# LN1's g and b behind the transpose, FFN2's sums made of turned tiles, the last rows by column halves, in an order written by hand

## The chip, the cores and the metric

The kernel runs on one core of a Trainium2 chip. A core has five engines with a queue of instructions each: TensorE (PE; its weight loads are shown apart as PEld), VectorE (DVE), ScalarE (ACT), GpSimd (POOL) and SyncE (SP), which issues the DMAs here. Engines run side by side and wait for each other through semaphores. The metric is the device time of one execution in microseconds (us).

## The reference

One layer of an encoder over x of 1024 tokens by 1024 columns, all float32: a half-step FFN, then attention and a two-directional state-space scan (SSD) side by side, then a second FFN, then a gated embedding. Each step ends in a layer norm.

```python
def _layer_norm(x, g, b):
    mu = jnp.mean(xf, axis=-1, keepdims=True)
    var = jnp.mean(jnp.square(xf - mu), axis=-1, keepdims=True)
    return (xf - mu) * lax.rsqrt(var + LN_EPS) * g + b
...
x = _layer_norm(ALPHA * x + 0.5 * _swiglu(x, ffn1_w_in[i], ffn1_w_out[i]), ln_g[i, 0], ln_b[i, 0])
...
y = y.reshape(B, S, SSD_WIDTH) * jax.nn.silu(z)
y = _rms(y.reshape(B, S, G, SSD_WIDTH // G), 1.0).reshape(B, S, SSD_WIDTH)
mix = jnp.concatenate([att_out, y * ssd_norm[i]], axis=-1) @ w_out[i]
x = _layer_norm(ALPHA * x + mix, ln_g[i, 1], ln_b[i, 1])
x = _layer_norm(ALPHA * x + 0.5 * _swiglu(x, ffn2_w_in[i], ffn2_w_out[i]), ln_g[i, 2], ln_b[i, 2])
e = p[i] @ ple_w[i]
gate = jax.nn.sigmoid(x @ ple_gate_w[i] + ple_gate_b[i])
return _layer_norm(ALPHA * x + gate * e, ln_g[i, 3], ln_b[i, 3])
```

`_swiglu(x, w_in, w_out)` is `(silu(x @ gate) * (x @ up)) @ w_out` with 2816 hidden columns.

## The kernel before

The tokens are eight row tiles of 128. A float32 matrix product is made of three products of halves: each operand is split into a high part (a cast on ACT) and a low part (the difference, on DVE: `lo`, line 87), and TensorE adds hi x hi, lo x hi and hi x lo in PSUM (`mm3`, line 116). So every operand of a product costs one ACT and one DVE operation, and one product of 128x512 over four blocks is 12 matmuls.

The stages, in order of time: FFN1 (its in-products and its out-product), the projections, attention, the right scan (`ssd_right`), the left scan (`ssd_left`, line 1342), then LN1 and FFN2's in-products, FFN2's out-product (`ffn_strassen`, line 414), and the gate with LN3.

The left scan runs over eight chunks. For each, `load` brings y (the right scan's half, from DRAM) and silu(z); the state adds its part; y is gated, normed and, a few steps later, transposed by `turn` (four 128x128 transposes, line 1363) and split, as the second half of the input of W_out. Between the chunks stand "fillers": `resident(t)`, the attention half of W_out for rows 3 to 7, and `mixed(t)`, the SSD half (`out_proj`, two products of 128x512, line 1402) with LN1 of that row tile. `mixed(0)` to `mixed(4)` lie in the scan or right behind it, `mixed(5)` to `mixed(7)` among the work for FFN2. LN1 of a row tile is: statistics (on DVE, or on ACT by `ln_stats_act`), a root (on POOL, `ln_root`, line 175), and `ln_apply` (line 183): two DVE passes over 128x1024, with g and with b, which are held as 128x1024 tiles, the same in each partition. The result is stored to DRAM as y2, which FFN2's residual reads back later, and stays in `acc[t]` for FFN2.

FFN2's in-product is made in Strassen's way (Winograd's form) on 2x2 blocks. Rows 0 to 3 of x and rows 4 to 7 are the block rows, columns 0 to 511 and 512 to 1023 the block columns. Beside the plain blocks B11, B21 and B22 it needs sums T1 to T4 of blocks, all transposed and split. Before the change, `turn_blocks` transposes (line 237, into PSUM) first the plain blocks of rows 0 to 3, later the sums, which `Sums` makes on DVE out of rows of `acc` (lines 1639 to 1647), each sum of 128x512 with four transposes of its own. Hidden columns come in 22 blocks f; each has seven products: two "first" ones (with B11 and B21, which need only rows 0 to 3: `ffn_first`), and five of the "rest" (with T2, T1, T3, T4, B22: `ffn_rest`). The first products of f = 0, 1, 2 run ahead, between the rows. The weight sums of a block (`mixed_sums`, four of 128x512) are on DVE for f = 0 and on POOL for the others, and in each rest two sums of results (u2 and p5) are on POOL.

TensorE runs in the order in which the program is written. The other engines' order is a scheduler's, by its own estimates, except inside `in_order(...)`, where it is the written one, and `behind(...)`, which puts work behind what is already there. Waits lie at the head of each engine's queue.

The out-product `ffn_strassen` runs seven products of 22 steps; each step multiplies one hidden tile, whose splits run some tiles ahead on ACT and DVE. Pieces of DVE work (`todo`) are handed out two a step from step 3 on.

Of the kernel before, what the change touches and what calls it, by code (L numbers as in the profile page):

```python
# [36 lines left out]
class Layer:  # L37
# [62 lines left out]

    def split_into(self, b, src, n=512, eng=None):
        self.nc.scalar.copy(out=b[:, 0, :n], in_=src)  # L102
# [59 lines left out]
    def ln_stats_act(self, a, junk):

        nc = self.nc
        st = self.small.tile([P, 4, 6], F32, name="ln_st")[:, 0, 0:4]
        k = self.small.tile([P, 8], F32, name="ln_k")
        nc.scalar.activation(out=a, in_=a, func=AF.Identity, accum_out=st[:, 0:1])
        nc.scalar.mul(st[:, 1:2], st[:, 0:1], -1.0 / D)
        for i in range(2):
            nc.scalar.activation(out=junk, in_=a[:, i * 512:(i + 1) * 512], func=AF.Square, bias=st[:, 1:2], accum_out=st[:, 2 + i:3 + i])  # L170
        nc.vector.tensor_scalar(out=k[:, 0:1], in0=st[:, 0:1], scalar1=1.0 / D, scalar2=None, op0=ALU.mult)
        nc.vector.tensor_tensor(out=k[:, 1:2], in0=st[:, 2:3], in1=st[:, 3:4], op=ALU.add)
        return self.ln_root(a, k, k[:, 1:2], 1.0 / D)
# [53 lines left out]
    def put(self, X, name, k, c, src):  # L227
        hi, lo = X[name]
        self.nc.scalar.copy(out=hi[:, k, c], in_=src)
        self.lo(lo[:, k, c], src, hi[:, k, c])  # L230

    def turn_blocks(self, X, *blocks):

        ps = self.psb().rearrange("p (u k t) -> p u k t", u=2, t=P)
        for u, (_, _, src) in enumerate(blocks):
            for k in range(4):
                self.nc.tensor.transpose(out=ps[:, u, k], in_=src[:, k * P:(k + 1) * P], identity=self.ident)
        for u, (name, t, _) in enumerate(blocks):
            self.put(X, name, slice(0, 4), slice((t % 4) * P, (t % 4 + 1) * P), ps[:, u])
# [7 lines left out]
    def mixed_sums(self, g, u, tmp, G):  # L247

        a11, a12, a21, a22 = g[:, :512], g[:, 512:], u[:, :512], u[:, 512:]
        s1, s2, s3, s4 = (tmp.tile([P, 512], F32, name=f"s{i + 1}") for i in range(4))  # L250
# [3 lines left out]
        G.tensor_tensor(out=s4, in0=a12, in1=s2, op=ALU.subtract)
# [5 lines left out]
    def ffn_first(self, X, tmp, sg, g, between=None, mid=None, end=None):  # L260

        p1 = tmp.tile([P, 512], F32, name="p1")
        w = g if isinstance(g, list) else self.gate_blocks(g)
# [3 lines left out]
        for i, b in enumerate(("B11", "B21")):  # L270
# [1535 lines left out]
```

## Time and profile before

| | us |
|---|---|
| median of 3 runs | 1994.98 (1994.54 to 1996.11) |
| profiled run | 1995.66 |
| span of the profiled run | 1993.9 |
| mean granted TensorE clock | 0.996 of full speed |
| left scan | about 1138 to 1202 of the span |
| rows 5 to 7, sums, first rests of FFN2 | about 1202 to 1309 |
| FFN2's out-product | about 1680 to 1894 |

In the rows of the profile a line number is that of the kernel before; `out<-in` gives the names of the tiles without their numbers; `[2.07 <-DVE y L1392]` behind a row says that the engine had been idle for 2.07 us and what ended the wait. TensorE is busy for 98% of the span, so only few stretches show it idle; the longest of them are in the two middle rows of the table.

### The profile page before, as it was taken

How to read it: one execution, taken by the hardware profiler on the slowest of the kernel's cores; microseconds unless marked ns; L12 is line 12 of the kernel's file. 1: busy time of each engine (PE TensorE's matmuls, PEld its weight loads, DVE VectorE, ACT ScalarE, POOL GpSimd, SP SyncE). 2: the span in 40 equal slices, each digit the busy share in tenths (PEclk: the TensorE clock that was granted, in tenths of full speed). 3: DMA queues.
4: the chain of work that ended last, by engine and by line, in shares of the span. 5: the costliest groups of instructions: out<-in, count | busy, mean ns of one | idle time of the engine just before them, and what ended most of it. 6: DMA issues, size and time to landing. Idle time of an engine off the chain costs nothing.

```text
span 1993.9 us, 25875 instructions
## 1 busy us (share of the span) xinstructions
PE 1954.4 (98%) x9244; PEld 1622.9 (81%) x9244; DVE 1536.6 (77%) x2306; ACT 863.7 (43%) x1499; POOL 467.6 (23%) x338
## 2 busy tenths in 40 slices
PE   8999999999999999999999998899999999999998
PEld 7788888888888889877888877778888888888886
DVE  7977777766668668759997789877778777567698
ACT  6433333334444235448887664433333333443311
POOL 0544445430001131000001011354445441001011
PEclk9999999999999999999999999999999999999999
DMA  7434544559864202230003471234454447976122
GB/s 286 143 122 153 189 176 147 186 190 358 296 232 148 85 21 95 78 132 7 1 1 123 164 259 64 85 122 166 157 185 164 170 164 257 381 254 226 43 74 95
DMA packets 146605, 308.90 MB, mean 155 GB/s; under 512 B 17345, under 2 KB 30017, under 8 KB 146476
## 3 DMA queue, kind: packets, MB, share of 16 engines
q1 hardware_dynamic: 146476, 307.25, 43.8%
q8 instruction: 72, 1.18, 0.2%
q14 instruction: 57, 0.47, 0.1%
HBM read 215.77 MB, written 91.42 MB: 154 GB/s over the span
## 4 chain that ended last, share of the span: by engine, by line
PE 83%; DVE 10%; DMA 3%; issue 2%; ACT 2%; POOL 1%; SPq 0%; DVEq 0%; POOLq 0%; ACTq 0%
PE sm L116 48%; PE big L490 12%; PE sm L490 9%; PE big L116 3%; PE big L1102 2%; PE sm L1124 2%; DVE blk L87 2%; PE sm L1139 1%; PE sm L1140 1%; DMA wr<-in_wo_dram 1%; DVE nm L1109 1%; PE sm L1317 1%; DVE xl L87 1%; DMA wT<-wr 1%; PE sm L1213 1%
## 5 line engine op out<-in xcount | busy, mean ns | idle before, releaser
L116 PE MATMUL sm<-xh,blk 128*128 128x512 f32 x1424 | 439.8, 389 | 0.0
L116 PEld LDWEIGHTS sm<-xh,blk 128*128 128x128 f32 x1424 | 267.5, 188 | 55.3
L116 PE MATMUL sm<-xl,blk 128*128 128x512 f32 x736 | 284.6, 390 | 0.0
L116 PE MATMUL sm<-blk,xl 128*128 128x512 f32 (+2 forms) x784 | 238.2, 371 | 0.2 <-ACT xn_t L955 0.2
L116 PE MATMUL sm<-blk,xh 128*128 128x512 f32 (+2 forms) x584 | 203.8, 380 | 0.1
L87 DVE TENSOR_TENSOR blk<-raw,blk 128x512 fp32r<-128x512 f32 (+1 forms) x174 | 175.0, 1015 | 36.0 <-ACT blk L102 35.4
L102 ACT CAST blk<-raw 128x512 fp32r<-128x512 f32 (+1 forms) x174 | 104.6, 611 | 216.7 <-PE sm L116 119.9
L179 POOL TENSOR_TENSOR ln_k<-ln_k,mhalf 128x1 f32<-128x1 f32 x32 | 39.8, 1248 | 591.2 <-DVE ln_k L178 590.3
L87 DVE TENSOR_TENSOR blk<-s,blk 128x512 fp32r<-128x512 f32 x176 | 152.5, 872 | 28.6 <-ACT blk L102 28.1
L102 ACT CAST blk<-s 128x512 fp32r<-128x512 f32 x176 | 107.2, 622 | 137.4 <-PE sm L116 113.0
L116 PEld LDWEIGHTS sm<-blk,xl 128*128 128x128 f32 x784 | 142.8, 188 | 24.2 <-ACT xn_t L955 0.5
L116 PEld LDWEIGHTS sm<-xl,blk 128*128 128x128 f32 x736 | 138.3, 188 | 29.2 <-DVE u L370 0.4
L490 PE MATMUL big<-xh 128*128 128x512 f32 x576 | 138.8, 390 | 0.0
L251 POOL TENSOR_TENSOR s<-raw 128x512 f32<-128x512 f32 x41 | 62.0, 1512 | 323.7 <-DVE blk L87 272.0
L87 DVE TENSOR_TENSOR xh<-blk,xh 128x1024 fp32r<-128x1024 f32 x78 | 95.3, 1222 | 51.2 <-ACT xh L438 40.6
L87 DVE TENSOR_TENSOR xl<-blk,xl 128x1024 fp32r<-128x1024 f32 x76 | 92.8, 1221 | 47.2 <-ACT xl L438 39.6
L490 PEld LDWEIGHTS big<-xh 128*128 128x128 f32 x576 | 107.8, 188 | 22.2
L438 ACT CAST xh<-blk 128x1024 fp32r<-128x1024 f32 x78 | 82.2, 1054 | 100.8 <-PE big L490 37.6
L116 PEld LDWEIGHTS sm<-blk,xh 128*128 128x128 f32 x584 | 109.8, 188 | 19.7 <-DVE blk L87 0.5
L438 ACT CAST xl<-blk 128x1024 fp32r<-128x1024 f32 x76 | 80.1, 1054 | 104.4 <-PE big L490 38.5
L490 PE MATMUL big<-xl 128*128 128x512 f32 x480 | 115.7, 390 | 0.0
L116 PE MATMUL sm<-xET2h,blk 128*128 128x512 f32 x352 | 109.8, 394 | 1.8 <-DVE blk L87 1.8
(330 smaller groups left out, 4066.0 us busy)
## 6 DMA issues: line engine op xcount, KB each, us to landing
raw<-in_wi_dram SPq DMA_DIRECT2D x84, 512.0 KB
blk<-hS SPq DMA_DIRECT2D x154, 256.0 KB
hS<-h SPq DMA_DIRECT2D x88, 256.0 KB
wr<-in_wo_dram SPq DMA_DIRECT2D x44, 512.0 KB
blk<-wT SPq DMA_DIRECT2D x88, 256.0 KB
hS<-sg SPq DMA_DIRECT2D x66, 256.0 KB
wT<-wr SPq DMA_DIRECT2D x66, 256.0 KB
blk<-in_wo_dram SPq DMA_DIRECT2D x66, 256.0 KB
```

Source lines behind the costliest of these rows:

```text
L87: (eng or self.nc.vector).tensor_tensor(out=out, in0=full, in1=hi.bitcast(F32), op=ALU.subtract)
L102: self.nc.scalar.copy(out=b[:, 0, :n], in_=src)
L116: self.nc.tensor.matmul(ps, lhsT=a, rhs=b, start=(i == 0), stop=(i == n - 1))
L179: nc.gpsimd.tensor_tensor(out=r, in0=v, in1=self.mhalf[:, :1], op=ALU.pow)
L251: G.tensor_tensor(out=s1, in0=a21, in1=a22, op=ALU.add)
L438: A.copy(out=b[:, :, 0], in_=r)
L490: nc.tensor.matmul(ps[q], lhsT=b[:, 0, x, cut], rhs=b[:, 1, y], start=j == i == 0, stop=j == NP - 1 and i == 2)
L1102: nc.tensor.matmul(ps[:, n * 512:(n + 1) * 512], lhsT=Q[:, h, q0:q0 + P], rhs=K[:, h // 4, j, n * 512:(n + 1) * 512], start=j == 0, stop=j ...
L1109: nc.vector.tensor_reduce(out=nm, in_=ps, axis=AX.X, op=ALU.max, negate=True)
L1124: nc.tensor.transpose(out=pt[:, k], in_=pr[:, kk * P:(kk + 1) * P], identity=self.ident)
L1139: nc.tensor.matmul(po, lhsT=vw, rhs=pth[k // 4][:, k % 4], start=k == 0, stop=False)
L1140: nc.tensor.matmul(po, lhsT=vw, rhs=ptl[k // 4][:, k % 4], start=False, stop=k == KD - 1)
```

## The change

1. LN1 no longer multiplies by g and adds b on rows. `Row.shift` is one ACT pass (scale and shift by the row's own factors); the rows go to DRAM so.
2. `flip(t)` transposes two raw rows at once (rows 6 and 7 alone), and ACT's eviction out of PSUM carries g and b, which are one number per partition there (`gT`, `bT`), eight pieces of 128x256 for a pair. The turned tiles overwrite `acc[t]` and `acc[t + 1]`.
3. All blocks and sums are then made of turned tiles in SBUF (`plain`, `Sums`), with no transpose of their own: 64 transposes of 128x128 in place of 112.
4. What was stored without g and b gets them in FFN2's out-product (`affine`: 32 operations of 128x512 on DVE, in the steps of products 1 to 3), out of 128x1024 tiles that are now loaded there.
5. Statistics are on DVE for all rows. Rows 5, 6 and 7 run by column halves: 5 left, 5 right, 6 left, 7 left, 6 right, 7 right.
6. ACT's and DVE's order from row 5 to the third first product is written by hand. The sums u2 and p5 of f = 0 and the weight sums of f = 1 move from POOL to DVE.
7. In the left scan, y of chunks 0 and 1 is loaded ahead, and a `turn` comes behind the next chunk's state steps.
8. The attention stage's reciprocal of 128x512 is cut in four.

```diff
@@ ln
+    def ln_shift(self, a, k):
+        self.nc.scalar.activation(out=a, in_=a, func=AF.Identity, scale=k[:, 6:7], bias=k[:, 7:8])
+
+    def ln_factors(self, k):
+        V = self.nc.vector
+        mv, r, h, t, s, m = k[:, 0:2], *(k[:, i:i + 1] for i in range(3, 8))
+        V.scalar_tensor_tensor(out=t, in0=r, scalar=h, in1=r, op0=ALU.mult, op1=ALU.mult)
+        V.scalar_tensor_tensor(out=s, in0=t, scalar=1.5, in1=r, op0=ALU.add, op1=ALU.mult)
+        V.scalar_tensor_tensor(out=m, in0=mv[:, 0:1], scalar=-1.0, in1=s, op0=ALU.mult, op1=ALU.mult)
@@ ffn_strassen
+        made_of = {1: ("11",), 2: ("12",), 3: ("21", "22")}
...
-            todo = [(t, i, q) for t, i in adds[p] for q in range(4)]
+            todo = [do for to in made_of.get(p, ()) for do in affine(*C[to])]
+            todo += [lambda a=(t, i, q): add(*a) for t, i in adds[p] for q in range(4)]
@@ ffn_y
+        def affine(t0, m):
...
+            for t in range(t0, t0 + 4):
+                for gb, op in zip(xgb, (ALU.mult, ALU.add)):
+                    yield lambda a=acc[t][:, m], gb=gb, op=op: V.tensor_tensor(out=a, in0=a, in1=gb[:, m], op=op)
@@ z_last
-            V.reciprocal(e, e)
+        def invert(m):
+            V.reciprocal(e[:, m], e[:, m])
@@ ssd_left
         load(0)
+        load(1)
         waiting = []
         for ch in range(NT):
-            if ch < NT - 1:
-                load(ch + 1)
...
                 st = self.next_state(two, st, 0, ch, xb)
+            if len(waiting) > 2:
+                turn(*waiting.pop(0))
+            if 0 < ch < NT - 1:
+                load(ch + 1)
...
-            if len(waiting) > 2:
-                turn(*waiting.pop(0))
@@ layer
-        lnp = self.load_ln(1, lp)
+        gT, bT = (self.const.tile([P, KD], F32, name=n) for n in ("gT", "bT"))
...
+        def flip(t, n=2, to=None):
...
+            for u in range(n):
+                for k in range(KD):
+                    nc.tensor.transpose(out=ps[k // 4][:, k % 4, u * P:(u + 1) * P], in_=acc[t + u][:, k * P:(k + 1) * P], identity=self.ident)
+            for k in range(KD):
+                nc.scalar.activation(out=to[k // 4][:, k % 4], in_=ps[k // 4][:, k % 4], func=AF.Identity, scale=gT[:, k:k + 1], bias=bT[:, k:k + 1])
...
-            self.ssd_left(c, loaded, late, mixT, fillers + [lambda: mixed(3), lambda: mixed(4)])
+            self.ssd_left(c, loaded, late, mixT, fillers + [lambda: mixed(3), lambda: (flip(0), mixed(4))])
...
-            plain(0)
-            plain(1)
-            mixed(5)
-            plain(2)
-            plain(3)
-            mixed(6)
-            sums(4)
-            apply7 = mixed(7)
-            sums(5)
+            flip(2)
...
+            with self.in_order(mybir.EngineType.Activation, mybir.EngineType.DVE):
+                plain(0)
+                plain(2)
...
+                r6.half(1)
+                r6.root()
+                flip(4)
+                later(*lo1)
+                r6.factors()
+                r6.shift()
+                r7.half(1)
+                r7.root()
...
+                t14 = s[4].one()
+                r7.factors()
+                r7.shift()
+                t24 = s[4].two()
+                t15 = s[5].one()
+                t25 = s[5].two()
+                p0 = first(w0, lambda: None)
+                later(*lo2, t24, t25, t14)
+                pre.append(self.first_kept(tmp, sgs[0], p0))
+                flip(6, 1, [acc[6][:, m] for m in (lo, hi)])
...
+                p1 = first(w1, lambda: flip(7, 1, [acc[7][:, m] for m in (lo, hi)]))
...
+                in_turn([s[t].three for t in range(4, NT)])
...
+                in_turn([s[t].four for t in range(4, NT)])
```

What this does to the order is best seen at three places. First, SP's queue ahead of the left scan, before (`acc1<-y1` brings back rows 0 to 2, `y2<-yd` the scan's y; ln_g and ln_b are LN1's two 128x1024 tiles):

```order
L1589 DMA acc1_10887<-y1_9639 128x1024
L1589 DMA acc1_10959<-y1_9639 128x1024
L148 DMA ln_g_10279<-in_ln_g_dram 128x1024
L149 DMA ln_b_10280<-in_ln_b_dram 128x1024
L1355 DMA y2_10288<-yd_9641 128x512
L1355 DMA y2_10292<-yd_9641 128x512
```

and with the change:

```order
L1622 DMA acc1_10887<-y1_9642 128x1024
L1622 DMA acc1_10959<-y1_9642 128x1024
L1385 DMA y2_10288<-yd_9644 128x512
L1385 DMA y2_10292<-yd_9644 128x512
L1385 DMA y2_10384<-yd_9644 128x512
L1385 DMA y2_10462<-yd_9644 128x512
L1220 DMA xb_10547<-xbn_6850 128x768
```

The two broadcast tiles are gone from here; they now stand in FFN2's out-product. Second, DVE around the statistics of row 7 (`acc1_10660`), before (xt2 is a sum of row 5, the `big` tiles are PSUM, `blk` the low parts of weights):

```order
L157 BN_STATS ln_st_11350<-acc1_10660 128x6
L178 TENSOR_SCALAR ln_k_11276<-ln_k_11276 128x1
L87 TENSOR_TENSOR xET3l_11127<-big_11376,xET3h_11126 128x4x128
L159 BN_AGGR ln_k_11353<-ln_st_11350 128x2
L180 TENSOR_SCALAR ln_k_11276<-ln_k_11276 128x1
L87 TENSOR_TENSOR xET2l_11125<-big_11362,xET2h_11124 128x4x128
L178 TENSOR_SCALAR ln_k_11353<-ln_k_11353 128x1
L193 SCALAR_TENSOR_TENSOR ln_k_11276<-ln_k_11276 128x1
L190 SCALAR_TENSOR_TENSOR acc1_10660<-acc1_10660,ln_k_11353,ln_g_10279 128x512 x2
L87 TENSOR_TENSOR xl10_11133<-big_11376,xh10_11132 128x4x128
```

and with the change:

```order
L1440 SCALAR_TENSOR_TENSOR acc1_10660<-sm_11350,acc1_10660 128x512
L167 BN_STATS ln_st_11208<-acc1_10660 128x6
L171 BN_AGGR ln_k_11365<-ln_st_11208 128x2
L177 TENSOR_SCALAR ln_k_11365<-ln_k_11365 128x1
L179 TENSOR_SCALAR ln_k_11365<-ln_k_11365 128x1
L1696 TENSOR_TENSOR acc1_10785<-acc1_10404,acc1_10785 128x4x128
L193 SCALAR_TENSOR_TENSOR ln_k_11365<-ln_k_11365 128x1
L194 SCALAR_TENSOR_TENSOR ln_k_11365<-ln_k_11365 128x1
L195 SCALAR_TENSOR_TENSOR ln_k_11365<-ln_k_11365 128x1
L1696 TENSOR_TENSOR u3_11376<-acc1_10482,acc1_10785 128x512
```

The wide passes with ln_g have gone, and the sums T1 and T2 of rows 4 and 5 (line 1696) now stand behind row 7's statistics. Third, DVE around the low parts of T4 (`xl11`), which the fourth product of the first rest reads, before (L1647 is the last of the sums T4; the two rows that follow the last one here repeat it for the right half):

```order
L276 TENSOR_TENSOR sg_11148<-p1_11517,sm_11550 128x512
L1647 TENSOR_TENSOR acc1_10296<-acc1_10296,xt2_11507 128x512
L87 TENSOR_TENSOR blk_11579<-s3_11511,blk_11579 128x512
L87 TENSOR_TENSOR blk_11582<-blk_11144,blk_11582 128x512
L363 TENSOR_TENSOR u2_11603<-p1_11391,sm_11606 128x512
L87 TENSOR_TENSOR blk_11585<-s4_11512,blk_11585 128x512
L87 TENSOR_TENSOR xl11_11390<-big_11620,xh11_11389 128x4x128
L87 TENSOR_TENSOR xl11_11390<-big_11633,xh11_11389 128x4x128
```

and with the change (L1696 are the sums T4):

```order
L87 TENSOR_TENSOR blk_11551<-s3_11246,blk_11551 128x512
L87 TENSOR_TENSOR blk_11554<-s4_11247,blk_11554 128x512
L1696 TENSOR_TENSOR acc1_10887<-acc1_10887,u3_11376 128x4x128
L1696 TENSOR_TENSOR acc1_10887<-acc1_10887,u2_11377 128x4x128
L372 TENSOR_TENSOR u2_11584<-p1_11422,sm_11587 128x512
L87 TENSOR_TENSOR xl11_11197<-acc1_10887,xh11_11196 128x4x128
L1696 TENSOR_TENSOR acc1_10296<-acc1_10296,h3_11487 128x4x128
L87 TENSOR_TENSOR xl11_11197<-acc1_10887,xh11_11196 128x4x128
L1696 TENSOR_TENSOR acc1_10296<-acc1_10296,p5_11488 128x4x128
L378 TENSOR_TENSOR u3_11585<-u2_11584,sm_11623 128x512
L87 TENSOR_TENSOR xl11_11197<-acc1_10296,xh11_11196 128x4x128 x2
L87 TENSOR_TENSOR xl10_11151<-acc1_10482,xh10_11150 128x4x128 x2
```

The low parts read SBUF (`acc1`) where they read PSUM (`big`) before; two of T4's four come behind `u3`, which needs the T3 product, and the low parts of B22 (`xl10`) follow.

More of the change, by code (lines that the diff above doesn't have):

```diff
@@ L157, in ln_stats, with ln_part, ln_rest @@
             nc.vector.bn_stats(st[:, i], a[:, i * size:(i + 1) * size])
+        return self.ln_rest(st, a)
+    def ln_part(self, st, a, i):
+        self.nc.vector.bn_stats(st[:, i], a[:, i * 512:(i + 1) * 512])
+    def ln_rest(self, st, a):
         k = self.small.tile([P, 8], F32, name="ln_k")
-        nc.vector.bn_aggr(k[:, 0:2], st)
+        self.nc.vector.bn_aggr(k[:, 0:2], st)
         return self.ln_root(a, k, k[:, 1:2], 1.0)
[L162 to L173, printed above, removed]
     def ln_root(self, a, k, var, scale):
@@ L227, in put, with put_later @@
     def put(self, X, name, k, c, src):
+        self.put_later(X, name, k, c, src)()
+    def put_later(self, X, name, k, c, src):
         hi, lo = X[name]
         self.nc.scalar.copy(out=hi[:, k, c], in_=src)
[L230 to L239, printed above, removed]
+        return lambda: self.lo(lo[:, k, c], src, hi[:, k, c])
     def product(self, w, x):
@@ L1400, in ssd_left, with out_proj @@
             turn(*w)
-    def out_proj(self, t, half, wm, mixT, a):
+    def out_proj(self, t, half, wm, mixT, a, ns=(0, 1)):
         nc = self.nc
-        for n in range(2):
+        for n in ns:
             m = slice(n * 512, (n + 1) * 512)
@@ L1700, in run, with __init__, one, two @@
-            lctx.close()
-            tmp.more()
+                def __init__(s, t, t2):
+                    s.t, (s.a12, s.a22), (s.a11, s.a21), s.t2 = t, F[t], F[t - 4], t2.rearrange("p (k t) -> p k t", t=P)
+                def one(s):
+                    sub(s.a11, s.a12, s.a11)
+                    return put("T1", s.t, s.a11)
+                def two(s):
+                    sub(s.t2, s.a22, s.a11)
+                    return put("T2", s.t, s.t2)
+                def three(s):
+                    sub(s.a12, s.a22, s.a12)
+                    return put("T3", s.t, s.a12)
@@ new lines, in four, with last, in_turn, gate @@
+                def four(s):
+                    sub(s.a21, s.a21, s.t2)
+                    return put("T4", s.t, s.a21)
+                def last(s):
+                    return put("B22", s.t, s.a22)
+            def in_turn(steps):
+                waiting = None
+                for step in steps:
+                    do = step()
+                    if waiting:
+                        waiting()
+                    waiting = do
+                waiting()
+            def gate(g):
+                return zip(*[self.split_later(g[:, m]) for m in (lo, hi)])
@@ L1702, in run, with rests @@
+            blocks0 = [blocks0[i] for i in range(5)]
+            g1, u1 = w(1, 0), w(1, 1)
+            mark = []
+            def rests():
+                with self.behind(mybir.EngineType.Activation), self.behind(mybir.EngineType.DVE):
+                    in_turn([s[t].last for t in range(4, NT)])
+                mark.append(self.last(mybir.EngineType.DVE))
             hS, store = self.left_factors(1, tmp)
-            self.ffn_rest(X, tmp, lambda h: store(0, h), blocks0, *pre[0], between=last_sums)
+            self.ffn_rest(X, tmp, lambda h: store(0, h), blocks0, *pre[0], between=(rests,), G=V)
@@ L1707, in run @@
             _, wT, steps = self.right_sums(xc, 1, I["wo2"])
-            self.ffn_h(X, I["wi2"], tmp, store, pre, 1, steps)
+            self.ffn_h(X, I["wi2"], tmp, store, pre, 1, steps, mark[0], (g1, u1))
         with ExitStack() as c:
             rctx.close()
-            acc, xT, wg, tp, turn = self.ffn_y(c, 2, lambda t: y2[t], hS, I["wo2"], wT, [I["wg"][0, k] for k in range(4)])
+            acc, xT, wg, tp, turn = self.ffn_y(c, 2, lambda t: y2[t], hS, I["wo2"], wT, [I["wg"][0, k] for k in range(4)], xln=1)
             self.gate(c, xT, turn, acc, wg, self.load_ln(3, tp, ("s1", "s2")))
```

210 lines of the change are left out of this document (123 added, 87 removed).

## The prediction, on record before the run

> **What bounds the kernel now.** I first read the page: engine totals and the shares of the chain that ended last.
>
> ```profile
> PE 1954.4 (98%) x9244; PEld 1622.9 (81%) x9244; DVE 1536.6 (77%) x2306; ACT 863.7 (43%) x1499; POOL 467.6 (23%) x338
> PE 83%; DVE 10%; DMA 3%; issue 2%; ACT 2%; POOL 1%; SPq 0%; DVEq 0%; POOLq 0%; ACTq 0%
> ```
>
> TensorE sets the time; what can be won is its waits, its slow clock and its own instructions. So I next read the busy times by window for the stretch that the change rewrites (columns: window, us, busy time and count of PE, PEld, DVE, ACT, POOL, then TensorE's granted clock, DMA share, GB/s), with one window of FFN2's out-product for comparison.
>
> ```profile
> 1155.00:1202.00 47.00, 44.82 (x203) 36.91 (x202) 42.06 (x106) 26.70 (x98) 6.39 (x8) 0.96 0.60 202
> 1202.00:1256.00 54.00, 48.15 (x244) 39.02 (x242) 53.47 (x117) 26.02 (x59) 7.51 (x8) 1.00 0.17 69
> 1256.00:1287.00 31.00, 26.77 (x131) 22.31 (x132) 21.52 (x34) 12.50 (x23) 6.04 (x5) 0.94 0.23 85
> 1287.00:1309.00 22.00, 19.45 (x84) 15.48 (x83) 20.67 (x22) 9.39 (x15) 17.68 (x12) 0.99 0.37 120
> 1309.00:1330.00 21.00, 21.00 (x87) 17.19 (x86) 18.05 (x23) 8.17 (x14) 10.93 (x8) 0.93 0.43 151
> 1700.00:1750.00 50.00, 50.00 (x222) 41.42 (x221) 31.64 (x35) 24.04 (x27) 0.00 (x0) 1.00 0.99 365
> ```
>
> Between 1155 and 1309 PE idles 47.00 - 44.82 + 54.00 - 48.15 + 31.00 - 26.77 + 22.00 - 19.45 = 14.8 us, and VectorE is full there (53.47 of 54, 20.67 of 22). Third, the waits of PE from 1205 to 1320, grouped (in total, times, longest), and one row of the chain of waits at the worst of them, the store that the sum waits for:
>
> ```profile
> PE big L237 <- DVE xt L1644: 7.1, 4, 2.5
> PE sm L116 <- DVE sg L371: 2.6, 2, 2.3
> PE big L237 <- DVE acc L1640: 1.3, 2, 0.7
> PE sm L1363 <- DVE y L1392: 1.2, 1, 1.2
> ...
> 1253.72 2.64 DMA y<-acc
> ```
>
> 8.4 of these 12.4 us are transposes that wait for the sums of LN1's rows (xt, acc): row, statistics, LN1, store, sum, transpose, in a chain that lies on DVE. Before them stands one wait in the left scan. These rows also mark the ends of my sum:
>
> ```profile
> 1161.98 1.08 PE L1363 MATMUL sm<-ident,y 128*128 128x128 f32 x4 [2.07 <-DVE y L1392]
> 1201.36 0.60 PE L1363 MATMUL sm<-ident,y 128*128 128x128 f32 x4
> 1270.65 0.47 PE L116 MATMUL sm<-xET2l,blk 128*128 128x512 f32 x1 [0.24 <-issue]
> 1308.57 0.68 PE L116 MATMUL sm<-xET2l,blk 128*128 128x512 f32 x1 [2.29 <-DVE sg L371]
> ```
>
> 1201.36 is the transpose of scan chunk 5; 1308.57 is the first product (T2) of the third FFN2 block's rest. **All sums below go against the profiled run, 1995.66 us (span 1993.9 and 1.8 around it); the median of the three runs, 1994.98, is 0.7 lower.** About 0.2% (4 us) is what a measurement of this kernel can tell from no change.
>
> **The change, part by part.** *Left scan.* The 1 MB of broadcast g and b leaves the queue ahead of the scan's y loads, and the first turn goes behind two more steps of the scan:
>
> ```profile
> 1145.16 0.33 SPq L148 DMA_DIRECT2D ln_g<-in_ln_g_dram  x1
> 1145.54 0.43 SPq L149 DMA_DIRECT2D ln_b<-in_ln_b_dram  x1
> 1146.01 3.22 SPq L1355 DMA_DIRECT2D y<-yd  x4
> ```
>
> That is worth what the window 1155 to 1202 loses: 2.18 us idle and 0.04 x 47 = 1.9 us of clock (0.96). Taken: 4.1; bounds 0 (the wait only moves) and 4.1.
>
> *PE's work from chunk 5's transpose to the third rest.* I price it by pitch, from start to start:
>
> ```profile
> 1215.75 1.91 PE L237 MATMUL big<-ident,acc 128*128 128x128 f32 x16
> 1217.41 0.48 PE L116 MATMUL sm<-blk,xh 128*128 128x512 f32 x1
> ...
> 1281.05 0.39 PE L116 MATMUL sm<-xl,blk 128*128 128x512 f32 x1
> 1286.49 0.40 PE L116 MATMUL sm<-xET2l,blk 128*128 128x512 f32 x1
> ```
>
> 16 transposes take 1.66 us (0.104 each); two products of 12 matmuls take 5.44 (2.72 each). After the change there stand, to the first rest: five rows of out-projection, ten products, 27.2; six first products, 16.3; 64 transposes of rows (96 before), 6.7; three turns of four, 1.2: 51.4 us, where the rows 1201.36 and 1270.65 show 69.3. Then twelve products, 32.7, with none of today's 16 transposes of T4. Sum 84.1, if PE never waits; before: 1308.57 - 1201.36 = 107.2.
>
> *DVE's work against it.* Removed: 14 passes of LN1. Added: 8 statistics, 6 sums that POOL did. The sums and low parts stay as many.
>
> ```profile
> L198 DVE SCALAR_TENSOR_TENSOR acc<-acc,ln_k,ln_b 128x1024 f32<-128x1024 f32 x7 | 8.9, 1278 | 0.1
> L190 DVE SCALAR_TENSOR_TENSOR acc<-acc,ln_k,ln_g 128x1024 f32<-128x1024 f32 x7 | 8.9, 1276 | 0.0
> L193 DVE SCALAR_TENSOR_TENSOR ln_k<-ln_k 128x1 f32<-128x1 f32 x8 | 1.7, 208 | 0.0
> ...
> 1276.62 0.68 DVE L87 TENSOR_TENSOR blk<-s,blk 128x512 fp32r<-128x512 f32 x1
> 1277.22 2.03 DVE L87 TENSOR_TENSOR xl<-big,xh 128x512 fp32r<-128x512 f32 x3
> 1260.91 0.69 DVE L87 TENSOR_TENSOR xET2l<-big,xET2h 128x512 fp32r<-128x512 f32 x1 [0.65 <-ACT xET2h L229]
> ```
>
> Back to back a 512-wide operation costs 0.60 (1276.62 to 1277.22), so DVE loses 17.8 and gains 14 x 0.60 = 8.4. Up to row 5 I find DVE early enough that PE does not wait. From the second half of row 7 on, everything left is written behind it: up to the last low part of T4's tiles DVE has 46 wide operations, 27.6, six small ones, about 0.9, and some four waits for ACT's high parts like the 0.65, 2.6: 31.1. PE has, from the same point to T4's product, nine products (24.5) and 16 transposes (1.7): 26.2. So a **new wait of 4.9** stands at T3 and T4. Behind it, DVE has 12 operations (7.2) up to the second block's first low part, PE two products (5.44): another 1.8. PE's stretch becomes 84.1 + 6.7 = 90.8, a gain of 16.4. Bounds for the waits: 0 (gain 23.1) and the 12.6 that this stretch idles today.
>
> *Clock.* The window 1309 to 1330 loses 0.07 x 21 = 1.5 us behind the 2.29 us wait. I let that go and set 1.5 again behind T4's wait: 0.
>
> By the Trainium skill, "TensorE: Matmul & The Clock Gate", Part 1, the clock falls only after about 3.4 us without work; by that rule T4's wait, if it reaches 3.4, would cost the same, and 2 us waits nothing. The windows at 0.93 to 0.96 behind waits of 2.07 to 2.54 us speak against the second half.
>
> *ACT.* LN1's rows become one Identity of 128x1024 each, and 40 small evictions with scale and bias carry g and b.
>
> ```profile
> L1386 ACT ACTIVATE ysq<-y 128x256 f32<-128x256 f32 x16 | 6.5, 407 | 5.3 <-DVE rs_t L124 4.6 <-DVE y L1382 0.5
> L1207 ACT ACTIVATE state<-state,cd 128x64 f32<-128x64 f32 x32 | 8.1, 335 | 3.0 <-DVE state L1230 3.0
> ```
>
> A pair's eight cost between 8 x 0.335 = 2.7 and 8 x 0.407 = 3.3. ACT is half idle (26.02 of 54), but each eviction also waits for the row's store (2.64 above), and by my count rows 2 and 5 have only 0.6 us to spare. I charge 1.0; bounds 0 and 3 x 0.6 + 1.5 of clock = 3.3.
>
> By the Trainium skill, "ScalarE: Activation LUTs", What ACT_TABLE_LOAD costs, each 128x1 operand adds about 93 ns to 186 ns + 0.833 ns per element: an estimate of 0.49 for 128x256 once overlap is taken off, 3.9 a pair. That would make the 1.0 some 2.5 and the time 1979.5; no row here has this form.
>
> *POOL and DVE together.* Today's low parts slow down beside POOL's sums, one whose source is in PSUM does not:
>
> ```profile
> 1285.44 4.52 DVE L87 TENSOR_TENSOR blk<-s,blk 128x512 fp32r<-128x512 f32 x3 [3.50 <-ACT blk L102]
> 1289.88 1.78 DVE L87 TENSOR_TENSOR blk<-raw,blk 128x512 fp32r<-128x512 f32 x1
> 1291.58 0.68 DVE L371 TENSOR_TENSOR sg<-u,sm 128x512 f32<-128x512 f32 x1
> ...
> 1285.96 1.75 POOL L254 TENSOR_TENSOR s<-raw,s 128x512 f32<-128x512 f32 x1
> ```
>
> 1.5 to 1.78 instead of 0.60. Two such operations stand before the second block's product: 1.8 charged; bounds 0 and ten operations, 9.
>
> *FFN2's out-product.* 32 operations of 0.60 = 19.2 us put g and b on y2 again; 1 MB more is loaded, at the 365 GB/s of the window 1700 to 1750 2.9 us of DMA.
>
> ```profile
> 1719.88 1.23 DVE L87 TENSOR_TENSOR xl<-blk,xl 128x1024 fp32r<-128x1024 f32 x1 [1.50 <-ACT xl L438]
> ```
>
> DVE idles 1.50 in every step of 2.72, two operations (1.2) fit in, and the splits run six tiles ahead (16.3 us); PE idles 0 there. Cost 0; without cover up to 19. A g that lands 2.9 us late would hold DVE for as long, out of those 16.3.
>
> *Attention.* One reciprocal becomes four pieces between which DVE can serve PE:
>
> ```profile
> 900.00:950.00 50.00, 46.43 (x262) 37.66 (x261) 49.94 (x70) 41.15 (x77) 3.50 (x4) 1.00 0.02 7
> 909.12 3.34 DVE L992 RECIPROCAL blk<-blk 128x512 f32<-128x512 f32 x1
> 913.07 0.66 PE L1124 MATMUL sm<-ident,pr 128*128 128x128 f32 x4 [2.05 <-DVE xh L87]
> ```
>
> The 2.05 us may go, but DVE has the same work and is busy for 49.94 of 50 us there, so it comes back at the next tile. Gain 0 to 2, taken 0.
>
> **Sum:** 4.1 + 16.4 + 0 - 1.0 - 1.8 = 17.7; 1995.66 - 17.7 = **1978**.
>
> **Rivals.**
> 1. *The written order costs more (1983 to 1990, say 1986).* The low parts of rows are now made from SBUF, not PSUM, and DVE is full from row 7 to the second rest. If the third block's sums run on POOL meanwhile, ten operations cost 9 us more instead of 1.8: 1985, with 1.5 of clock 1987. For: 17.68 of 22 busy on POOL at 1287. Against: six sums leave POOL, and its rest starts only when raw tiles land.
> By the Trainium skill, "GPSIMD Engine Reference", 1. Specifications, GpSimd shares SBUF interfaces with VectorE and contends when VectorE reads two SBUF inputs: 1285.44 and 1291.58 agree, and the rule speaks against this change.
> 2. *All waits go:* 4.1 + 23.1 + 1.5 = 28.7, 1967. It needs DVE 6.7 us earlier than I count.
> 3. *It doesn't do what it says:* LN1's wide passes leave DVE, but row 7's chain (matmul, statistics, POOL's root, ACT, store, flip) is as long as before, and the waits stay with new names. Left: transposes 48 x 0.104 = 5.0 less the 3.3 of ACT: 1994.
> 4. *Slower:* FFN2's out-product loses its cover. If the 32 operations run at the 1.78 us that low parts reach beside other traffic, 57 us stand against 16 x 1.50 = 24 of idle and 16.3 of lead: 16.7 late, 1995; if DVE's order lets it use none of the idle, 40.7, 2019. It decides above 17.7 late, 1.82 us an operation. Against it: POOL does nothing at 1700 to 1750, so only DMA is beside it.
>
> **How the numbers follow.** Forecast (1971 to 1983) 0.55; rival 1 0.22; rival 2 0.08; rival 3 0.08; rival 4 0.07. The range takes the forecast and rival 1, 1971 to 1989. Faster by over 4 us (below 1991): forecast, rivals 1 and 2, 0.85; within: 0.08; slower: 0.07.
>
> **What would show it.** Right: no wait at the turn near 1160 and a clock of 1.00; no wait at any flip; a wait of 3 to 5 us before the T3 or T4 product and a smaller one at the second block; first rest some 18 + 4 us earlier; PE idle 0 in FFN2's out-product with 32 operations at 0.60 to 0.7. Wrong: waits at flips of more than 1 us (ACT or stores), a DVE that idles while T4 is late, low parts at 1.5 in a row, or PE idle behind g's landing.

## The result, and the profile after

The changed kernel takes 1981.88 us (median of 4 runs, 1981.27 to 1982.73) against 1995.55 for the kernel before on the same chip: a ratio of 0.9932, 95% interval 0.992 to 0.9943, or 13.7 us less. The profiled run took 1981.3 us with a span of 1979.5, 14.4 below the span before. The forecast was 1978, the range 1971 to 1989.

The page's engine totals and the shares of the chain that ended last, after:

```profile
PE 1947.1 (98%) x9192; PEld 1617.6 (82%) x9196; DVE 1540.5 (78%) x2337; ACT 878.5 (44%) x1515; POOL 461.2 (23%) x332
PE 86%; DVE 7%; ACT 2%; issue 2%; POOL 1%; DMA 1%; SPq 0%; DVEq 0%; POOLq 0%; ACTq 0%
```

TensorE has 7.3 us less to do, VectorE about as much as before (3.9 more). The prediction's windows again, now after the change, in the same columns:

```profile
1155.00:1202.00 47.00, 47.00 (x223) 39.38 (x222) 44.58 (x120) 29.04 (x101) 6.87 (x10) 1.00 0.59 205
1202.00:1256.00 54.00, 50.75 (x256) 42.14 (x255) 45.03 (x100) 39.81 (x72) 4.76 (x6) 0.99 0.23 88
1256.00:1287.00 31.00, 27.03 (x101) 21.35 (x100) 30.67 (x47) 18.51 (x31) 7.77 (x5) 0.86 0.23 84
1287.00:1309.00 22.00, 22.00 (x98) 18.21 (x97) 20.77 (x23) 7.31 (x12) 16.17 (x11) 1.00 0.43 153
1309.00:1330.00 21.00, 21.00 (x94) 17.41 (x93) 14.43 (x20) 7.01 (x12) 11.91 (x8) 1.00 0.32 106
1700.00:1750.00 50.00, 50.00 (x222) 41.42 (x221) 44.13 (x59) 21.22 (x23) 0.00 (x0) 1.00 0.92 326
```

TensorE no longer idles in the scan's window (47.00 of 47) nor from 1287 on, and not in the out-product although VectorE does 12.5 us more there. What is left stands from 1251 to 1269, with a clock of 0.86 behind it, and VectorE is then full (30.67 of 31). TensorE's waits from 1150 to 1320, grouped, and the rows that mark the ends:

```profile
PE sm L122 <- DVE xl L87: 4.0, 1, 4.0
PE sm L122 <- ACT blk L104: 2.7, 1, 2.7
PE sm L122 <- DVE blk L87: 0.4, 1, 0.4
...
1198.74 0.60 PE L1393 MATMUL sm<-ident,y 128*128 128x128 f32 x4
1254.06 0.50 PE L122 MATMUL sm<-xET2l,blk 128*128 128x512 f32 x1 [2.70 <-ACT blk L104]
1268.81 0.79 PE L122 MATMUL sm<-xl,blk 128*128 128x512 f32 x1 [3.97 <-DVE xl L87]
1277.27 0.39 PE L122 MATMUL sm<-xET2l,blk 128*128 128x512 f32 x1
1296.31 0.39 PE L122 MATMUL sm<-xET2l,blk 128*128 128x512 f32 x1
```

The 12.4 us of waits from 1205 on have become 7.1: one ahead of the first rest's T2 product (1254.06), one ahead of T4 (1268.81). With these marks and the same ones before (attention starts at 881.96 and now 884.30, the scan's first state product stands at 1096.36 and 1098.07), the 14.4 us split up as follows:

| stretch | before | after | difference | forecast |
|---|---|---|---|---|
| start to attention | 882.0 | 884.3 | +2.3 | 0 |
| attention, right scan | 214.4 | 213.8 | -0.6 | 0 |
| left scan, to chunk 5's transpose | 105.0 | 100.7 | -4.3 | -4.1 |
| to the third rest | 107.2 | 97.6 | -9.6 | -12.1 |
| third rest to the end | 685.3 | 683.2 | -2.1 | -1.5 |

(The forecast's -16.4 for the fourth stretch is shown with the 1.0 and 1.8 that it charged elsewhere and with its 1.5 us of clock.) So two things are to be explained: 2.5 us less than forecast won in the rows and sums, and 2.3 us lost where nothing was changed.

### The profile page after: what moved, and what is told of

Read it like the earlier page. It is cut to its first block, busy times and chain, and to the rows that moved or that the text cites. A ratio compares the mean times of both kernels' runs of the same rounds, so it can differ in the third digit from the quotient of the medians.

```text
span 1979.5 us, 25793 instructions
## 1 busy us (share of the span) xinstructions
PE 1947.1 (98%) x9192; PEld 1617.6 (82%) x9196; DVE 1540.5 (78%) x2337; ACT 878.5 (44%) x1515; POOL 461.2 (23%) x332
## 4 chain that ended last, share of the span: by engine, by line
PE 86%; DVE 7%; ACT 2%; issue 2%; POOL 1%; DMA 1%; SPq 0%; DVEq 0%; POOLq 0%; ACTq 0%
PE sm L122 52%; PE big L505 12%; PE sm L505 9%; PE big L122 3%; PE big L1132 2%; PE sm L1154 2%; PE sm L1169 1%; PE sm L1170 1%; DVE nm L1139 1%; POOL qr L826 1%; PE sm L1347 1%; ACT acc L1662 1%; PE sm L1243 1%; DVE ptl L87 1%; PE sm L1254 1%
```

## Experiments

All are made from the changed kernel, the three with the sums earlier and with VectorE's help from the one with the inputs last. "Stretch" is from chunk 5's transpose to the third rest, read from one profile. Six of the profiled kernels, the changed one among them, have the same order there and show 96.4 to 97.6 (97.6 in the changed one's); the others are held against these two ends. Times are medians of 4 runs (5 for the filler); the kernel before took 1994.5, 1996.2 and 1994.9 us in the three sets.

### ACT's 16 small evictions

```diff
+            if n == 1:
+                for h in range(2):
+                    nc.scalar.copy(out=to[h], in_=ps[h])
+                return
```

> The changed kernel, but the turned tiles of rows 6 and 7 leave PSUM in two plain copies of 128x512 a row instead of eight scaled 128x128 pieces; g and b are left out of these two rows' input to FFN2. ACT theory (the 16 pieces, 5.69 us in the changed kernel, hold back the sums T1 and T2 and the first weight sums' high parts): ACT is some 3.5 us earlier, the wait of 2.70 before the first rest's first product falls to 0.5 or less, its slow clock goes with it, T4's wait stays near 4, the time is 3 to 5 us below the changed kernel's 1981.9. DVE theory (VectorE's count alone sets this stretch): the 2.70 shrinks, but T4's 3.97 grows by as much, and the time stays within 1 us of 1981.9.

Measured: 1981.22 us, ratio 0.9938 (0.9921 to 0.9955); stretch 94.95. Its waits, from TensorE's timeline:

```profile
1251.00 0.49 PE L122 MATMUL sm<-xET2l,blk 128*128 128x512 f32 x1 [1.26 <-ACT blk L104]
1265.69 0.50 PE L122 MATMUL sm<-xl,blk 128*128 128x512 f32 x1 [3.92 <-DVE xl L87]
```

and from ACT's:

```profile
1246.12 0.62 ACT L247 CAST xET1h<-acc 128x512 fp32r<-128x512 f32 x1 [2.07 <-DVE acc L1700]
```

The wait at T2 falls by 1.4, not by 2.7, T4's stays: ACT holds this place back, and behind ACT there is a second limit 1.4 us further on. It is VectorE, for which ACT now waits 2.07 us. The stretch is 1.5 to 2.6 shorter; the median doesn't show it, and the interval allows it. 1.5 is the better figure: the two products T4 and B22 take 7.21 us here, as much as in the profile with 96.4 that has the inputs last (7.20), and 8.46 in the one with 97.6.

### A product to fill T4's wait

```diff
+        if G is V:
+            self.idle_product(b3, X["T3"])
```

> The changed kernel, with one more product of 12 matmuls behind the first rest's T3 product, whose result nobody reads: TensorE is busy for 2.7 of the 4.0 us in which it waited for T4. Clock theory (the T4 and B22 products take 8.46 us instead of 5.44 because TensorE has been idle): the wait shows as about 1.3, the two products take 5.4 to 6, and the time falls by 2.5 to 3.5 us, to about 1979. Rival (DVE is the limit, so whatever PE wins at T4 it loses at the second block, where 12 DVE operations of 0.60 stand against 5.44 us of products): a new wait of about 1.8 there, and a gain of 1.2 or less.

Measured: 1986.58 us, ratio 0.9963 (0.995 to 0.9976); stretch 98.4. The edit also puts such a product into the first and last blocks of FFN1 (a mark behind them at 702.11 moves to 704.52) and into the last block of FFN2 (from its T2 product to the out-product 16.32 us instead of 13.60). These 5.1 us are more than the 4.7 by which the median lies above the changed kernel's. The rows of the second block:

```profile
1276.01 0.39 PE L122 MATMUL sm<-xET2l,blk 128*128 128x512 f32 x1
1278.25 0.72 PE L122 MATMUL sm<-xET2h,blk 128*128 128x512 f32 x2 [1.85 <-DVE blk L87]
```

The second block begins 75.6 us behind chunk 5's transpose instead of 77.0 to 78.5 (the six again): 1.4 to 2.9 us won on the clock, as the clock theory has it. Then it waits 1.85 us for the low part of its first weights, with a slow clock behind, and all is lost again. The T4 product itself starts 70.0 us behind chunk 5's transpose, as in the changed kernel (70.1). So both theories held a part: the slow clock costs its time at T4, and VectorE needs that time.

### Four splits left out

```diff
-                for i in (0, 1):
-                    blocks0[i], do = self.split_later(left[i])
-                    do()
+                blocks0[0] = blocks0[1] = blocks0[3]
...
+                blocks0[2] = blocks0[4] = blocks0[3]
```

> The changed kernel, but the first rest uses one split block of the weight sums for all its five products: four high parts (ACT) and four low parts (DVE) are left out, so the products are of the wrong sums. DVE theory: T4's low parts come 4 x 0.60 = 2.4 us earlier, T4's wait falls from 3.97 to about 1.6 or, with the wait ahead of it also gone, stays near 3; the time falls by 4 to 6 us with the clock. ACT theory: the 2.70 wait ends two casts earlier (about 1.0) and goes to 1.7 or, since the weight's high part is what it waited for, to 0.

Measured: 1980.55 us, ratio 0.9931 (0.9916 to 0.9946); stretch 96.0.

```profile
1253.87 0.47 PE L122 MATMUL sm<-xET2l,blk 128*128 128x512 f32 x1 [2.42 <-ACT p L283]
1266.44 0.50 PE L122 MATMUL sm<-xl,blk 128*128 128x512 f32 x1 [2.55 <-DVE xl L87]
1274.26 0.74 PE L122 MATMUL sm<-xET2h,blk 128*128 128x512 f32 x2 [1.84 <-DVE blk L87]
```

This kernel multiplies the wrong weight sums. T4's wait falls by 1.4 and the one at T2 by 0.3 with the weights gone from ACT's way: T2 did not wait for the weights as such, they were the last thing in ACT's queue. T4's product starts 67.6 us behind chunk 5's transpose instead of 70.1: 2.4 us, what four low parts take at 0.60, as the VectorE theory has it. T4 and B22 then run without a slow clock (5.57 us), and the wait of the second block shows here too, with a slow clock behind it: from T4 to the third rest it takes 28.4 us instead of 26.4 to 27.5. The gain in the stretch, 0.4 to 1.6, is well below the 4 to 6 expected of the time.

### Rows 6 and 7 whole

```diff
                 r6.half(0)
                 sums[2]()
-                r7.half(0)
                 sums[3]()
...
+                r7.half(0)
                 r7.half(1)
```

> The changed kernel, but row 7's left columns come behind row 6's right ones: rows 5, 6, 7 run whole. If the order by column halves is needed: rows 4 and 5 are turned one product (2.7 us) earlier, the transposes wait 1 to 2 us for row 5's ACT pass, row 7's statistics come no earlier, and the time rises by 1 to 4 us over 1981.9. If it is not needed, because TensorE waits only for T2 and T4 later: within 1 us of 1981.9 or slightly below.

Measured: 1982.99 us, ratio 0.9943 (0.9928 to 0.9958); stretch 98.5.

```profile
1229.30 1.09 PE L1660 MATMUL big<-ident,acc 128*128 128x128 f32 x8 [2.83 <-ACT acc L188]
1255.41 0.51 PE L122 MATMUL sm<-xET2l,blk 128*128 128x512 f32 x1 [1.40 <-ACT blk L104]
```

The transposes of row 5 wait 2.83 us for its ACT pass, as expected, and the wait at T2 gets 1.3 shorter for it. T4's product starts 1.4 us later (71.5 behind chunk 5's transpose); the order by halves is worth 0.9 to 2.1 us of the stretch. The median lies 1.1 above the changed kernel's; the intervals overlap.

### The 1 MB ahead of the scan, and the transposes' place

```diff
+        self.load_ln(1, lp)
```

> The changed kernel, with the two 128x1024 broadcasts of ln_g and ln_b loaded again ahead of the left scan's y, as in the kernel before (nothing reads them). From the scan's first state product on the slowest stage ahead of chunk 5's transpose takes 100.7 us in the changed kernel (1098.07 to 1198.74) and 105.0 before (1096.36 to 1201.36). Queue theory (the 1 MB held back y): 102.5 to 105, a wait of 1 to 2 us at the first transpose, time 2 to 4 us above the changed kernel's 1981.9. Order theory (it is the transpose that now stands behind two more steps of the scan): 100.7, no wait, time unchanged.

```diff
         load(0)
-        load(1)
...
+            if ch < NT - 1:
+                load(ch + 1)
...
                 fillers.pop(0)()
+            if len(waiting) > 2:
+                turn(*waiting.pop(0))
```

> The changed kernel, with the scan's transposes and loads at their old places (transpose at the end of a chunk's step, next chunk's load at its head), and still without the 1 MB ahead of them. Queue theory: 100.7 to 102 us from the first state product to chunk 5's transpose, no wait at the first transpose or under 0.5. Order theory: 103 to 105, a wait of about 2 at the first transpose and its slow clock, time 2 to 4 us up. If both causes do the same thing twice, each of these two kernels stays near 100.7 alone.

Measured: with the loads 1985.67 us, ratio 0.9954 (0.9938 to 0.9969), and 105.2 us from the first state product (1098.01) to chunk 5's transpose; with the old order 1982.31, ratio 0.9929 (0.9907 to 0.995), and 102.1 us (from 1097.29). The kernel with the loads first, then that with the old order:

```profile
1165.74 0.85 PE L1393 MATMUL sm<-ident,y 128*128 128x128 f32 x4 [2.47 <-DVE y L1425]
1203.18 0.60 PE L1393 MATMUL sm<-ident,y 128*128 128x128 f32 x4
```

```profile
1184.17 0.50 PE L122 MATMUL sm<-blk,xh 128*128 128x512 f32 x1 [1.10 <-DVE blk L87]
1199.43 0.60 PE L1393 MATMUL sm<-ident,y 128*128 128x128 f32 x4
```

The loads alone bring back the wait at the first transpose and the whole 4.3 us. The old order alone brings no wait there; it costs 1.5 us by another one, at 1184. The 1 MB ahead of y is the cause; whether by its place in the queue or by the DMA time that it takes was not tried.

### Twice the work on y2

```diff
-                for gb, op in zip(xgb, (ALU.mult, ALU.add)):
+                for gb, op in 2 * list(zip(xgb, (ALU.mult, ALU.add))):
...
+            pace = 4 if len(todo) > 15 else 2
```

> The changed kernel, with g and b put on y2 twice in FFN2's out-product (64 operations instead of 32, four a step instead of two; the second pass makes the residual another one than the reference's). Cover theory (VectorE idles 1.50 in a step of 2.72 and the splits lead by 16.3 us): four operations are 2.4 in a step, 0.9 late a step over 16 steps is 14.4, with the 6.2 us that VectorE waits for the loads of g, b and y 20.6: TensorE waits 2 to 5 us in the out-product, time up by 2 to 6. If the cover is larger than I count: no wait and no change. In the changed kernel itself the cover holds either way.

Measured: 1984.06 us, ratio 0.9942 (0.9925 to 0.9959). The out-product in the window view, and in the changed kernel the group of the first operations (line, form, count, busy, mean ns, idle before):

```profile
1750.00:1800.00 50.00, 50.00 (x222) 41.44 (x221) 50.00 (x67) 21.09 (x23) 0.00 (x0) 1.00 0.79 261
```

```profile
L539 DVE TENSOR_TENSOR acc<-acc,ln_g 128x512 f32<-128x512 f32 x16 | 10.6, 685 | 6.2 <-DMA ln_b<-in_ln_b_dram 3.8 <-DMA acc<-y 2.4
```

With 64 operations, which leave a wrong residual, VectorE is full for a whole window while TensorE never waits, there or elsewhere in the out-product (190.00 of 190 us busy from 1690 to 1880); the cover is larger than I counted. In the changed kernel VectorE stood 6.2 us for the loads of b and y without a mark on TensorE. (The 2.2 us by which the median lies higher stand elsewhere, in one wait of 2.2 us at 1508 among the in-products and the slow clock behind it. Waits for the same operation of VectorE there, of 0.4 to 2.3 us in all, are in seven of the 13 profiles of the changed kernel and its variants, 1.65 us at 1512 in the one with the 1 MB, and not in the changed kernel's; their cause is open, and they are a part of what the medians of two variants differ by.)

### Where the new inputs lie

```diff
-    for n in "gb":
-        A[f"ln1_{n}T"] = ...
...
+    for n in "gb":
+        A[f"ln1_{n}T"] = ...
     return A
```

> The changed kernel, with the two new small inputs (g and b of LN1, 128x8) declared behind all others instead of in the middle; the program is the same, only where the inputs lie in DRAM changes. Placement theory (all five profiles of the changed program's family show the attention's norm weights w_q and ws_q landing 1.5 to 2.7 us later than before, with small TensorE waits at 754 to 772 behind them): they land at about 709.4 again, the attention starts at 882 instead of 884.3, and the time falls by about 2 us. Chance or another cause: the attention starts at 884 again and the time stays within 1 us.

Measured: 1979.59 us, ratio 0.992 (0.9905 to 0.9935). VectorE's row that waits for w_q in the changed kernel, with TensorE's wait behind it:

```profile
710.96 0.69 DVE L815 SCALAR_TENSOR_TENSOR T<-cs,w_q 128x512 f32<-128x512 f32 x1 [5.12 <-DMA w_q<-in_qn_dram]
766.18 1.06 PE L882 MATMUL big<-ident,qs 128*128 128x128 f32 x8 [0.63 <-DVE qs L87]
```

and with the inputs last:

```profile
709.00 0.69 DVE L815 SCALAR_TENSOR_TENSOR T<-cs,w_q 128x512 f32<-128x512 f32 x1 [3.74 <-DMA ws_q<-in_qns_dram]
```

The attention starts at 881.53, TensorE's waits at 766 and 771 are gone. From a transpose at 702 to the attention's start it is 180.0 us before and 180.0 here; in all nine profiles with the inputs in the middle 181.7 to 182.2, in all four with them last 180.0 to 180.3. The placement is the cause of 2 us; what in it makes the loads land later, no view shows.

### Versions with the sums earlier, and with VectorE's help

```diff
-                plain(0)
-                plain(2)
+                left, sums = self.mixed_steps(g0, u0, tmp, V)
+                plain(0, sums[:2])
+                plain(2, sums[2:])
...
+                blocks0[0], do = self.split_later(left[0])
...
                 in_turn([s[t].four for t in range(4, NT)])
+                blocks0[4], do = self.split_later(left[4])
+                do()
```

> The kernel with the inputs declared last (1979.6), and the first block's four weight sums moved ahead to rows 0 to 3, where VectorE waits 0.85 to 1.53 us for ACT three times; two of its splits follow behind rows 5 and 6, one goes behind T4. All of the reference is computed. DVE theory: three low parts fewer (1.8 us) stand between row 7 and T4, T4's wait falls from 3.97 to 2 to 2.6, the wait ahead of T2 stays at 2 or more because T2's own low parts still come behind the 16 evictions on ACT; chunk 5's transpose to the third rest 1.5 to 3 us shorter than 96.4, time 1976.5 to 1978.5. If ACT alone sets the stretch: within 1 us of 1979.6.

```diff
+                if n == 1 and k >= 5:
+                    nc.vector.tensor_scalar(out=to[k // 4][:, k % 4], in0=ps[k // 4][:, k % 4], scalar1=gT[:, k:k + 1], scalar2=bT[:, k:k + 1], op0=ALU.mult, op1=ALU.add)
+                    continue
```

> The same, and three of the eight pieces of each of rows 6 and 7 leave PSUM by VectorE (a multiply and an add with a number per partition, 128x128) instead of ACT. If the 16 pieces on ACT (0.356 each) hold T2 back and VectorE only waits there (1.30 us): ACT is 2.1 us earlier, VectorE gets 6 operations of about 0.2, T2's wait falls to 0.5 to 1.5 and the stretch by another 1 to 2.5 us, time 1975 to 1977.5. If VectorE is the limit: T4's wait grows by what T2's loses and nothing is won over the kernel without it.

> The kernel with the inputs declared last, with VectorE's share of the evictions alone, sums where the change has them. ACT theory: T2's wait from 2.71 to about 1.3, T4's near 4 as it was; stretch 1 to 2 us below 96.4, time about 1978. DVE theory: T4's wait rises to 4.5 or more, no gain.

Measured: early sums 1977.57 us, ratio 0.9919 (0.9905 to 0.9934), stretch 94.3; with VectorE's share 1984.23, 0.9949 (0.9934 to 0.9964), stretch 98.6; the share alone 1982.28, 0.9934 (0.9917 to 0.995), stretch 96.9. First the rows with early sums, then those of the share alone:

```profile
1251.09 0.47 PE L122 MATMUL sm<-xET2l,blk 128*128 128x512 f32 x1 [1.29 <-ACT p L283]
1264.27 0.50 PE L122 MATMUL sm<-xl,blk 128*128 128x512 f32 x1 [3.42 <-DVE xl L87]
```

```profile
1243.99 1.04 DVE L1663 TENSOR_SCALAR acc<-big,gT,bT 128x128 f32<-128x128 f32 x3
1252.69 0.50 PE L122 MATMUL sm<-xET2l,blk 128*128 128x512 f32 x1 [3.17 <-ACT blk L104]
```

With early sums both waits shrink (2.70 to 1.29, where 2 or more was expected, and 3.97 to 3.42, where 2 to 2.6 was), the stretch by 2.1 against the kernel with the inputs last (96.4). This is the fastest version; against the one with the inputs last the intervals overlap. VectorE's share gains nothing: a piece takes 0.32 us there, not 0.2, so six of them take 1.9 where ACT was spared 2.1; VectorE's idle time is gone, and TensorE waits longer at T2 than before. T4's wait stays at 3.99, where the VectorE theory had 4.5 or more. With early sums and the share, the stretch's 4.3 more stand mostly behind T4: a wait of 1.76 us in the second block, and one of 2.89 ahead of the third rest for VectorE, which had itself waited 2.41 for POOL. (The 2.7 us by which the median of the share alone lies above that with the inputs last stand for the most part behind its stretch: its profile has 2.3 us of the waits among the in-products named above.)

### The reciprocal whole again

```diff
-        aside += [one_more, *(lambda m=slice(i * P, (i + 1) * P): invert(m) for i in range(4)), silu]
+        aside += [one_more, lambda: invert(slice(0, 512)), silu]
```

> The changed kernel with the attention stage's reciprocal whole again (one of 3.34 us). From the first score product to the last one the stage took 184.1 us before and 183.4 with the change; the wait of 2.05 at 913 went, and small waits of 0.6 came at 929, 939 and 955. If cutting the reciprocal does that: 184.0 to 184.2 here, with the 2 us wait back. If the stage's length comes from something else in the new order: 183.4.

Measured in one run with a profile: 1979.82 us; from the first score product to the last 183.6 us (883.25 to 1066.88).

```profile
915.23 0.66 PE L1154 MATMUL sm<-ident,pr 128*128 128x128 f32 x4 [0.97 <-DVE a_raw L1177]
916.95 0.66 PE L1154 MATMUL sm<-ident,pr 128*128 128x128 f32 x4 [1.07 <-DVE ptl L87]
```

The waits come back in two parts, but the stage is only 0.2 longer than with the pieces: the cut is worth next to nothing, and the other 0.5 us that the stage gained comes with the new order as such. Which part of it was not tried; nor was the scheduler's order for rows 5 to 7 in place of the written one, or the sums that left POOL put back on it.

## Why the prediction was right, and where its sizes were off

*Left scan.* Right in size (4.1, measured 4.3) and in cause: the 1 MB in the queue gives it back whole.

*TensorE's work.* The forecast had 84.1 us of work between the marks. The measured 97.6 are 84.1, the waits of 7.1, the slow clock of 4.8, and 1.6 of small gaps.

*T4's wait.* On the engine and at the operation named, and near in size: forecast 4.9 at T3 and T4, measured 3.97. But the size is luck. The step that did not hold is "PE has, from the same point to T4's product": the two engines are not at the same point. TensorE's first row behind its product for row 7's second half, and VectorE's operation that takes this product:

```profile
1233.07 0.39 PE L122 MATMUL sm<-xl,blk 128*128 128x512 f32 x1
...
1236.71 0.68 DVE L1440 SCALAR_TENSOR_TENSOR acc<-sm,acc 128x512 f32<-128x512 f32 x1
```

VectorE, whose timeline shows no pause since 1222, comes 3.6 us late. Its own work from there was counted well: T4's product starts 32.1 us on, counted were 31.1. So TensorE starts T4's product 9.5 us later than its 26.2 us of work alone would let it, not 4.9: 3.97 in front of it and the other 5.5 in the wait at T2, the slow clock and small gaps. All versions bear this out (row 7 is counted from chunk 5's transpose):

| kernel | VectorE takes row 7's second half | T4's product starts after that |
|---|---|---|
| changed; filler; 1 MB; twice the work; inputs last; reciprocal whole | 37.9 to 38.0 | 32.1 |
| old order in the scan | 37.3 | 32.1 |
| rows 6 and 7 whole | 39.4 | 32.1 |
| bulk eviction (VectorE's wait of 1.30 for ACT is gone) | 37.9 | 30.7 |
| four low parts fewer (2.4) | 37.9 | 29.7 |
| early sums (three low parts fewer, 1.8) | 36.5 | 30.3 |
| VectorE's share alone (1.9 more, the wait of 1.30 gone) | 38.0 | 32.6 |
| early sums and VectorE's share | 36.5 | 30.8 |

VectorE's queue sets T4's start. Up to there the stretch is 4.6 us longer than forecast (70.1 against 65.5: 84.1 less nine products, and the 4.9 and 1.0); behind it, it is 2.1 shorter (27.5 against 29.6). That the whole came within 2.5 us is in part luck, too. The first rest came 16.6 us earlier, not "some 18 + 4".

*The second block's wait.* Forecast 1.8, and 1.8 more for POOL; TensorE shows none. It is not gone, but covered: T4 and B22 ran at a low clock. These rows are a set of three matmuls each, from TensorE's timeline of the changed kernel:

```profile
1271.54 0.63 PE L122 MATMUL sm<-xl,blk 128*128 128x512 f32 x1
1272.82 0.63 PE L122 MATMUL sm<-xl,blk 128*128 128x512 f32 x1
...
1275.90 0.40 PE L122 MATMUL sm<-xl,blk 128*128 128x512 f32 x1
1276.59 0.39 PE L122 MATMUL sm<-xl,blk 128*128 128x512 f32 x1
```

1.28 us a set, then 0.69. From 1268.81 to 1277.27 it is 8.46 us for two products that take 5.44: 3.0 lost (1.5 to 3.0 in the six profiles of this order), and as much gained by VectorE. The filler, which takes the slow clock away, makes the wait appear, 1.85 us, as it was forecast, and so does leaving out the four splits, 1.84. In both, and with early sums, the row that had waited stands 7.82 us behind T4's first: VectorE's 12 operations, counted as 7.2.

*Clock.* This term was mis-sized: "I let that go and set 1.5 again behind T4's wait" had 1.5 for one wait; T4's cost 3.0 in this profile, and the one at T2 another 1.8 (its product takes 4.89 from 1254.06 on, 0.42 of that a second wait). No price for a wait fits all runs: behind 2.55 us ahead of T4 (four splits left out) the two products took 5.57 us, at a granted clock of 1.00, while behind 1.26 and 0.43 us at T2 (bulk eviction) one took 5.14, at 0.67. What decides it no run shows. By the Trainium skill, "TensorE: Matmul & The Clock Gate", Part 1, the clock falls after about 3.4 us without work; the slow rows behind 2.70 us here, and behind 2.29 before, come earlier than that.

*ACT.* "I charge 1.0" looked in the wrong place. No transpose waits (the flips show none), but the 16 pieces of rows 6 and 7 stand in ACT's queue ahead of T1's and T2's high parts. ACT's timeline, and VectorE's wait behind it:

```profile
1231.33 3.74 ACT L1662 ACTIVATE acc<-big,bT,gT 128x256 f32<-128x256 f32 x8
1243.62 5.69 ACT L1662 ACTIVATE acc<-big,bT,gT 128x128 f32<-128x128 f32 x16
1253.39 1.14 ACT L104 CAST blk<-s 128x512 fp32r<-128x512 f32 x2
...
1249.86 0.69 DVE L87 TENSOR_TENSOR xET1l<-acc,xET1h 128x512 fp32r<-128x512 f32 x1 [1.30 <-ACT xET1h L247]
```

A piece of 128x256 takes 0.47, one of 128x128 0.36; my bounds from the nearest rows were 0.34 and 0.41 for the former. I priced a pair's pieces and overlooked that rows 6 and 7, turned alone, need 16. What they cost is VectorE's wait of 1.30: evicting them in bulk lets T4's product start 1.5 us sooner, against the 1.0 charged. The 3.1 us of waits at T2 and the 1.8 of clock behind were not forecast, but lie within VectorE's 32.1 us: with the filler the T2 product took 0.9 longer still (5.78), and T4's started no later. By the Trainium skill, "ScalarE: Activation LUTs", What ACT_TABLE_LOAD costs, the pieces were estimated at 0.49; the trace agrees better with that than with my rows.

*POOL beside DVE.* The slow low parts came (two beside POOL's sums take 3.51 us together at 1279.43), and TensorE shows no wait behind them. Rival 1 named the right engines, but its cost did not come.

*FFN2's out-product.* Right: hidden, with more cover than counted. Rival 4 would have needed more than the 64 operations that were tried.

*A reading.* The passes that leave VectorE are more than the 14 counted: row 7's, in four halves of 128x512 (2.8 us), are in the profile too. No term of the sum rests on it.

*Attention and the start.* 0 was forecast for both. The 2.3 us lost ahead of the attention lay outside every step: the program there is the same, and where the inputs lie in DRAM is not in the order of instructions at all.

## What to carry to other kernels

When a stretch is bound by the sums behind TensorE, count the queue of each helper engine between two marks, and ask how far behind TensorE it already is at the first of them: VectorE's 31 us were counted to 1 us, and the 3.6 us by which it came late were not. Here relieving ACT gained only what VectorE had waited for it, relieving VectorE ahead of T4 was in part lost at the next block, and only work moved to where VectorE waited anyway (the early sums) won. A wait removed for TensorE may be another engine's time to catch up, so a price for it holds only until the next operation that this engine owes. And a kernel with new inputs should be compared stage by stage from its first instruction on: part of what it loses or wins may have nothing to do with the edit.
